# A ConvFFN's up projections by a seven-product scheme over token halves and gate/up columns, in a two-layer float32 decoder

## The chip, the cores and the metric

One core of one Trainium2 chip. The metric is the device time of one execution in microseconds. Before the change it is 1314.91 us, the median of 3 runs (1314.73 to 1315.43).

## What is computed

Two layers on 512 tokens of 1024 features, all float32. Layer 0 mixes by a Mamba-2 scan, layer 1 by differential attention, and behind each mixer stands the same kind of feed-forward block. The change lies in these two blocks alone:

```python
def conv_ffn(x, ln_g, up_w, conv_w, conv_b, down_w):
    u = causal_dwconv(rms_norm(x, ln_g) @ up_w, conv_w, conv_b)
    gate, up = u[..., :FFN_DIM], u[..., FFN_DIM:]
    return (jax.nn.silu(gate) * up) @ down_w
```

`FFN_DIM` is 2816, so `up_w` is 1024 x 5632 and `down_w` is 2816 x 1024 in each layer. `causal_dwconv` is three taps along the tokens and a bias.

## The kernel before

**Features on partitions.** In the feed-forward block every tensor lies with 128 features on the partitions and the 512 tokens along the row. The 2816 gate columns are 22 blocks of 128, and so are the up columns; block p of both makes "pair" p.

**Float32 by three products.** TensorE works on fp32r. Each operand is split into a high piece (ACT copies it to fp32r) and a low piece (DVE subtracts the high piece from the value). One product of values is three matmuls: high by high, high by low, low by high (`mm3`, lines 207 to 210). A weight chunk is 128 x 1024 values: SP loads it into one of three `raw` tiles (line 140), ACT makes `wh` (line 148), DVE makes `wl` (line 159), each from a pool of three buffers. The list `plan` holds all chunks in order of use, and `chunk()` (line 199) splits those up to two ahead of the one in use.

**The up projection** (`products`, line 1002). The chunk `g` or `u` of a pair holds 8 blocks of 128 x 128, one for each 128 input features. They are multiplied with `xgh` and `xgl`, the pieces of the residual stream times its gain; each of the 24 matmuls streams 512 tokens. The RMS factor of each token is not in them: `taps` (line 1013) multiplies the PSUM bank by the row `rr` on DVE while it empties it (line 1021), ACT starts the convolution (line 1022) and DVE does the two other taps (line 1024). The gate goes through Silu on ACT (line 1272), DVE multiplies it with the up half (line 1276).

**The down projection** already runs by a Strassen scheme, over pair parity, token halves and output columns: seven products in place of eight. `operands` (line 1097) makes, for two pairs together, seven 128 x 256 sides in high and low pieces. `down_features` (line 1209, layer 0) streams 256 tokens a matmul and takes the products in the order 5126743; `down_tokens` (line 1129, layer 1) takes 1257634. Sums of weights are made in place: `combine` (line 1065) splits a tile, and then a DMA from POOL adds the next summand to it in DRAM-to-SBUF accumulate mode (`plus`, line 1051). The 22 pairs are done in three parts, `PARTS_D = (0, 6), (6, 14), (14, 22)` (line 32): the up projection of a part, then its share of the down projection (loop at line 1265). In layer 0 the sides for products 5 and 1 need only the even pair of each two; the others also need the odd pair.

**Order.** Within the feed-forward blocks the instruction streams of the engines are put in order at build time by the framework's scheduler, which lets a later instruction go ahead of one whose inputs it does not take to be ready; on the chip each engine then runs its stream in that order. From pair 6 on, layer 0 also stages the scaled key weights for the next mixer (`key_weights_in`, `key_weights_out`, lines 965 and 972): eight loads of 512 KB, and eight stores. Two sets of four PSUM banks, `mm` and `aux`, serve as targets.

Of the kernel before, what the change touches and what calls it, by code (L numbers as in the profile page):

```python
# [18 lines left out]
P = 128  # L19
# [12 lines left out]
PARTS_D = (0, 6), (6, 14), (14, 22)  # L32
# [10 lines left out]
def trunk_kernel(ctx: ExitStack, tc, x, ssm_ln_g, ssm_in_w, ssm_conv_w, ssm_conv_b, ssm_dt_bias,  # L43
# [48 lines left out]
    def ffn_plan(l):  # L92
        for p0, p1 in PARTS_D:
            for p in range(p0, p1):
                plan.append(("g%d_%d" % (l, p), *w_cols(ffn_up_w[l], 0, KB, p * P, P)))
                plan.append(("u%d_%d" % (l, p), *w_cols(ffn_up_w[l], 0, KB, FFN + p * P, P)))
# [28 lines left out]
    state = {"next": 0, "use": 0}  # L125
# [3 lines left out]
    class Weights:  # L129


        def __init__(self, i, behind=None):
# [7 lines left out]
            sync.dma_start(self.cols(self.raw), src)  # L140
# [48 lines left out]
    def emit_chunk():  # L189
        i = state["next"]  # L190
        if i < len(plan):
            state["next"] = i + 1
            if len(plan[i]) == 2:
                state["combine"](plan[i][0], *plan[i][1][1:])
                return
            with tc.issue_after(state["rs"]) if i < 5 else nullcontext():
                Weights(i).split()
# [767 lines left out]
    def key_weights_in(pl, n, behind):  # L965
        t = pl.tile([P, 1024], F32, tag="stage", name="stage%d" % n, bufs=1)
# [31 lines left out]
    def ffn(l, norm, bp, gnext, nnext):  # L998
        with tc.tile_pool(name="ffn_h%d" % l, bufs=1) as hp, tc.tile_pool(name="ffn%d" % l, bufs=1) as fp:
            rr = []  # L1000

            def products(j, p, c=None):
                key = "%s%d_%d" % ("gu"[j], l, p)
                wh, wl = chunk(key)
                ps = mm_bank("ps_" + key)
                for k in range(KB):
                    last = mm3(ps, wh[:, k, :], wl[:, k, :], xgh[k], xgl[k], k == 0, k == KB - 1)
                    if c is not None and k == KB - 2:
                        with tc.issue_after(last):
                            rr.append(norm.row(c))  # L1010
                return ps

            def taps(j, p, ps):
                key = "%s%d_%d" % ("gu"[j], l, p)
                r = rr[0]
                col = lambda t: cf[l][:, 88 * j + 22 * t + p:88 * j + 22 * t + p + 1]
                u = fp.tile([P, T], F32, tag="u", name="u" + key, bufs=3)
                v = fp.tile([P, T], F32, tag="v%d" % j, name="v" + key, bufs=3 if j else 4)
                if nnext is None and key in ("g1_1", "u1_1"):
                    residual(j)  # L1020
                dve.tensor_tensor(out=u, in0=ps, in1=r, op=ALU.mult)  # L1021
                act.activation(v, u, AF.Identity, bias=col(3), scale=col(2))  # L1022
# [713 lines left out]
```

## Time and profile before

| | |
|---|---|
| median of 3 runs | 1314.91 us |
| the profiled execution | 1314.37 us |
| its span, first to last instruction | 1312.7 us |
| layer 0's feed-forward block in it | about 376 to 729 us |
| layer 1's feed-forward block in it | about 959 to 1312 us |
| granted TensorE clock | 1.000 |

The prediction shows the lines on which it rests. The busy time of an engine is the time in which at least one of its instructions was in flight; instructions overlap, so a duration and the distance to the next start differ. A line of a timeline gives the start, the duration, the engine, the line of the kernel, the operation, and output and inputs; in square brackets stands the idle time before it and what ended it.

### The profile page before, as it was taken

The page shows a single profiled execution, that of the slowest core. Times are in us where ns is not written, and L with a number is a line of the kernel's source. Part 1 is how long each engine was busy: PE and PEld are TensorE (multiplying, and loading weights), DVE is VectorE, ACT ScalarE, POOL GpSimd, SP SyncE. Part 2 cuts the span into 40 slices and gives each one's busy share as a digit, 9 for nine tenths or more (in the row PEclk, how much of TensorE's full clock was granted, in tenths as well). Part 3 has the DMA queues.
Part 4 walks back from the last instruction along what each step waited for, and adds up shares of the span by engine and source line. Part 5 has one row for each costly group of instructions (what it writes and reads, how often), then busy time and mean ns, then how long its engine had stood idle before and what let it go on. Part 6 is the DMA issues. An engine that isn't in the chain of part 4 may idle for free.

```text
span 1312.7 us, 18264 instructions
## 1 busy us (share of the span) xinstructions
PE 1307.3 (100%) x6771; PEld 1096.3 (84%) x6771; DVE 1073.9 (82%) x1774; ACT 713.9 (54%) x1156; POOL 177.1 (13%) x244
## 2 busy tenths in 40 slices
PE   9999999999999999999999999999999999999998
PEld 8878888888888998898889887777888888888887
DVE  7889878888888877876888878678778878887886
ACT  6696554743344545543556667777654544544452
POOL 5330200300021401020113210000020100010001
PEclk9999999999999999999999999999999999999999
DMA  7543533432234656774767763222225446453635
GB/s 210 161 152 87 151 99 108 140 96 82 88 91 137 126 144 200 177 163 121 206 174 150 190 131 114 80 65 69 61 81 160 101 116 191 98 96 113 193 64 128
DMA packets 202552, 167.84 MB, mean 128 GB/s; under 512 B 7580, under 2 KB 175904, under 8 KB 202464
## 3 DMA queue, kind: packets, MB, share of 16 engines
q1 hardware_dynamic: 176080, 124.93, 31.9%
q0 software_dynamic: 22928, 36.46, 14.8%
q10 hardware_dynamic: 3456, 5.30, 1.1%
q8 instruction: 53, 0.87, 0.3%
q14 instruction: 35, 0.29, 0.1%
HBM read 160.21 MB, written 6.44 MB: 127 GB/s over the span
## 4 chain that ended last, share of the span: by engine, by line
PE 99%; ACT 1%; DVE 0%; issue 0%; DVEq 0%
PE ps_g L209 6%; PE ps_u L208 6%; PE ps_g L208 6%; PE ps_u L210 6%; PE ps_g L210 6%; PE ps_u L209 6%; PE ps_in L208 5%; PE ps_in L210 5%; PE ps_in L209 5%; PE ps_s L1239 3%; PE ps_s L1244 3%; PE ps_s L1242 3%; PE ps_s L1146 3%; PE ps_s L1141 3%; PE ps_s L1144 3%; PE ps_o L209 2%
## 5 line engine op out<-in xcount | busy, mean ns | idle before, releaser
L208 PE MATMUL ps_u<-xgh,wh_u 128*128 128x512 f32 x352 | 137.4, 390 | 0.0
L209 PE MATMUL ps_g<-xgl,wh_g 128*128 128x512 f32 x352 | 137.2, 390 | 0.0
L208 PE MATMUL ps_g<-xgh,wh_g 128*128 128x512 f32 x352 | 137.0, 389 | 0.0
L210 PE MATMUL ps_u<-xgh,wl_u 128*128 128x512 f32 x352 | 137.0, 389 | 0.0
L210 PE MATMUL ps_g<-xgh,wl_g 128*128 128x512 f32 x352 | 137.0, 389 | 0.0
L209 PE MATMUL ps_u<-xgl,wh_u 128*128 128x512 f32 x352 | 136.9, 389 | 0.0
L208 PE MATMUL ps_in<-xgh,wh_in 128*128 128x512 f32 x304 | 123.0, 404 | 0.0
L210 PE MATMUL ps_in<-xgh,wl_in 128*128 128x512 f32 x304 | 119.7, 394 | 0.0
L209 PE MATMUL ps_in<-xgl,wh_in 128*128 128x512 f32 x304 | 119.2, 392 | 0.0
L209 PEld LDWEIGHTS ps_g<-xgl,wh_g 128*128 128x128 f32 x352 | 66.1, 188 | 14.3 <-DVE xgl L488 0.7
L210 PEld LDWEIGHTS ps_u<-xgh,wl_u 128*128 128x128 f32 x352 | 66.1, 188 | 13.8
L1244 PE MATMUL ps_s<-sl,wh_s 128*128 128x256 f32 x308 | 77.5, 283 | 0.0
L1242 PE MATMUL ps_s<-sh,wh_s 128*128 128x256 f32 x308 | 77.5, 283 | 0.0
L210 PEld LDWEIGHTS ps_g<-xgh,wl_g 128*128 128x128 f32 x352 | 66.1, 188 | 13.7
L208 PEld LDWEIGHTS ps_g<-xgh,wh_g 128*128 128x128 f32 x352 | 66.0, 188 | 13.6
L208 PEld LDWEIGHTS ps_u<-xgh,wh_u 128*128 128x128 f32 x352 | 66.1, 188 | 13.5
L209 PEld LDWEIGHTS ps_u<-xgl,wh_u 128*128 128x128 f32 x352 | 66.1, 188 | 13.5
L1052 POOL DMA_DIRECT2D wz<-in_ffn_down_w_dram x36 | 44.2, 1294 | 235.2 <-DVE wl_s L1080 167.4
L1126 ACT ACTIVATE sh<-vg 128x256 fp32r<-128x256 f32 (+1 forms) x44 | 23.0, 524 | 97.3 <-DVE vg L1276 97.3
L1272 ACT ACTIVATE vg<-vg 128x512 f32<-128x512 f32 x44 | 27.8, 633 | 78.4 <-DVE vg L1024 78.4
L1024 DVE SCALAR_TENSOR_TENSOR vg<-ug,cf,vg 128x511 f32<-128x511 f32 x88 | 65.8, 748 | 5.5 <-ACT vg L1022 4.1
L1021 DVE TENSOR_TENSOR uu<-ps_u,nr_f 128x512 f32<-128x512 f32 x44 | 30.4, 690 | 48.0 <-PE ps_u L210 48.0
(425 smaller groups left out, 3501.2 us busy)
## 6 DMA issues: line engine op xcount, KB each, us to landing
wr_g<-in_ffn_up_w_dram SPq DMA_DIRECT2D x44, 512.0 KB, 3.9
wr_u<-in_ffn_up_w_dram SPq DMA_DIRECT2D x44, 512.0 KB, 3.9
wr_in<-in_ssm_in_w_dram SPq DMA_DIRECT2D x40, 512.0 KB, 3.9
wz<-in_ffn_down_w_dram POOLq DMA_DIRECT2D x27, 512.0 KB, 5.9
m<-cumd POOLq DMA_DIRECT2D x16, 512.0 KB, 4.3
wr_out<-in_ssm_out_w_dram SPq DMA_DIRECT2D x16, 512.0 KB, 3.4
wr_s<-in_ffn_down_w_dram SPq DMA_DIRECT2D x13, 512.0 KB, 3.7
xT<-in_ffn_down_w_dram SPq DMA_DIRECT2D x10, 512.0 KB, 7.0
```

The lines of the kernel that those rows point to most:

```text
L208: pe.matmul(ps, wh, xh, start=start, stop=False)
L209: pe.matmul(ps, wh, xl, start=False, stop=False)
L210: return pe.matmul(ps, wl, xh, start=False, stop=stop).ins
L1021: dve.tensor_tensor(out=u, in0=ps, in1=r, op=ALU.mult)
L1024: dve.scalar_tensor_tensor(out=v[:, s:], in0=u[:, :T - s], scalar=col(2 - s), in1=v[:, s:], op0=ALU.mult, op1=ALU.add)
L1052: pool.dma_start(view(t, nq), source(p0, c, nq, j, i), accum_op=ALU.add)
L1141: pe.matmul(pss[b], h, ws[q][1][:, cols], start=False, stop=end and q == qs[-1], skip_group_check=more)
L1144: pe.matmul(pss[b], h, ws[q][0][:, cols], start=first and q == qs[0], stop=False, skip_group_check=more)
L1146: pe.matmul(pss[b], w, ws[q][0][:, cols], start=False, stop=False, skip_group_check=more)
L1239: pe.matmul(v[:, b], wl[:, q, cols], h, start=False, stop=q == nq - 1, skip_group_check=not opens or b > 0)
L1242: pe.matmul(v[:, b], wh[:, q, cols], h, start=opens and q + b == 0, stop=False, skip_group_check=not opens or b > 0)
L1244: pe.matmul(v[:, b], wh[:, q, cols], w, start=False, stop=False, skip_group_check=not opens or b > 0)
```

## The change

For pairs 6 to 21 two pairs are taken together ("double"). Their four blocks (two of gate, two of up) are computed by seven products over three splits: parity of the 128-feature input blocks, token halves, and gate or up columns. A product is one chunk (4 blocks of input features by 256 columns), multiplied with 256 tokens: 24 matmuls of 256 tokens, times seven. The order is 5126734. Sums and differences of the products are formed in PSUM (products 6, 7 and 4 add to the bank of 1, product 3 to that of 5) and by the instructions that empty the banks.

The inputs of this scheme are linear sums of x, so the token factor has to be in x: during pairs 0 and 1 x is multiplied by gain and `rr` (`normalised`) and split again into the same tiles `xgh` and `xgl` (`split_whole`), and during pairs 2 to 5 the sums of x are formed and split (`x_sums`, `last_sum`). Pairs 2 to 5 still run with 512 tokens a matmul but need no factor any more: their taps read PSUM directly. Pairs 0 to 5 take gate and up interleaved, in chunks of 4 blocks of input features for both (`whole`).

Four of the seven weight sums of a double are made by accumulating DMAs from POOL, as in the down projection: `up_ahead` loads and sums for the next double, `up_combine` splits and then issues the next summand. The parts are now (0, 6), (6, 12), (12, 18), (18, 22), so there is a fourth pass of the down projection. `operands` makes the sums in place in the gate tiles: in a double the even pair contributes its first side, and all sums come with the odd pair; in layer 0 sides 5 and 7 are split together, and 4 and 6 together; in layer 1 sides 6 and 7, and 3 and 5. The staged key weights use a `raw` tile; loads for the down projection hang on given chunks (`hooks`).

```diff
-PARTS_D = (0, 6), (6, 14), (14, 22)
+PARTS_D = (0, 6), (6, 12), (12, 18), (18, 22)
+WHOLE = 6
+STRASSEN_UP = "5126734"
...
+            def normalised(tmp):
+                for j, k, t in tmp:
+                    for i in range(2):
+                        b = 2 * (k + i) + j
+                        g = c2[:, (16 if l == 0 else 24) + b:(16 if l == 0 else 24) + b + 1]
+                        dve.scalar_tensor_tensor(out=t[:, i], in0=xT[b], scalar=g, in1=rr[0],
+                                                 op0=ALU.mult, op1=ALU.mult)
+            def split_whole(j, k, t):
+                pieces(*(x_[:, j, k:k + 2, :] for x_ in xside), t)
+            def x_sums(k, e, o):
+                e0, e1, o0, o1 = (t[:, :, h * 256:(h + 1) * 256] for t in (e, o) for h in range(2))
+                dve.tensor_tensor(out=e0, in0=e0, in1=e1, op=sub)
+                dve.tensor_tensor(out=e1, in0=o1, in1=e1, op=sub)
+                dve.scalar_tensor_tensor(out=o1, in0=o1, scalar=-1.0, in1=e0, op0=ALU.mult, op1=sub)
+                dve.scalar_tensor_tensor(out=o0, in0=o1, scalar=-1.0, in1=o0, op0=ALU.mult, op1=sub)
+                pieces(*(t[:, k:k + 2] for t in sE), e)
+                pieces(*(t[:, k:k + 2] for t in s1), o1)
...
+            def up_combine(key, m, p):
+                if m in "24":
+                    t = wrp.tile([P, 1024], F32, tag="raw", name="wr_" + key)
+                    sync.dma_start(up_view(t), up_source(p, 1, 0 if m == "2" else 1))
+                else:
+                    t = ups[p][m in "17"]
+                wh = wp.tile([P, 1024], F32R, tag="wh", name="wh_" + key)
+                wl = wp.tile([P, 1024], F32R, tag="wl", name="wl_" + key)
+                act.activation(wh, t, AF.Copy)
+                dve.tensor_tensor(out=wl, in0=t, in1=wh.bitcast(F32), op=sub)
+                ready.append((key, up_view(wh), up_view(wl)))
+                more = {"1": (0, 1), "5": (0, 0), "6": (1, 0)}.get(m)
+                if more:
+                    up_plus(t, p, *more)
...
+            def double(p, sides, meanwhile):
...
+                for m in STRASSEN_UP:
+                    wh, wl = chunk("U%d%s_%d" % (l, m, p))
...
+                    for b in range(2):
...
+                        for k in range(4):
+                            pe.matmul(ps[b], wh[:, k, cols], hs[:, k, :], start=not skip and k == 0, stop=False,
+                                      skip_group_check=skip)
+                            pe.matmul(ps[b], wh[:, k, cols], ls[:, k, :], start=False, stop=False,
+                                      skip_group_check=skip)
+                        for k in range(4):
+                            pe.matmul(ps[b], wl[:, k, cols], hs[:, k, :], start=False, stop=k == 3,
+                                      skip_group_check=skip)
+                        if m == "1":
+                            act.activation(ug[:, b, :256], ps[b], AF.Copy)
+                        elif m == "6":
+                            act.activation(ug[:, b, 256:], ps[b], AF.Copy)
+                        elif m == "7":
+                            dve.tensor_tensor(out=uu[:, b, 256:], in0=uu[:, b, 256:], in1=ps[b], op=sub)
+                        elif m == "4":
+                            act.activation(uu[:, b, :256], ps[b], AF.Copy, scale=-1.0)
+                    if m == "5":
+                        act.activation(uu[:, :, 256:], banks["yt"], AF.Copy, scale=-1.0)
+                    elif m == "2":
+                        dve.tensor_tensor(out=ug[:, :, :256], in0=banks["zt"], in1=ug[:, :, :256], op=ALU.add)
+                        meanwhile(ug)
+                    elif m == "3":
+                        dve.tensor_tensor(out=ug[:, :, 256:], in0=banks["yt"], in1=ug[:, :, 256:], op=ALU.add)
+                        ga = [taps(0, p + b, ug[:, b]) for b in range(2)]
+                        for b in range(2):
+                            act.activation(ga[b], ga[b], AF.Silu)
+                for b in range(2):
+                    gated(p + b, ga[b], taps(1, p + b, uu[:, b]), sides)
...
             def operands(p, ga, sides):
...
+                    pieces(sh[:, 0], sl[:, 0], h[:, 0])
+                    return
+                sh, sl, e = sides[-1]
+                pieces(sh[:, 1:3], sl[:, 1:3], h)
...
+                pieces(sh[:, 3:5], sl[:, 3:5], e)
+                pieces(sh[:, 5:7], sl[:, 5:7], h)
...
-                side = {"1": 0, "2": 1, "4": 2, "5": 3, "6": 4, "7": 5, "3": 6}
+                side = {"1": 0, "2": 1, "4": 2, "6": 3, "7": 4, "3": 5, "5": 6}
...
-                side = {"1": 0, "2": 1, "3": 2, "5": 3, "6": 4, "7": 5, "4": 6}
+                side = {"1": 0, "2": 1, "3": 2, "5": 3, "7": 4, "4": 5, "6": 6}
...
+            ps0 = whole(0)
+            ps1 = whole(1)
+            u0 = evac(0, ps0)
...
+            normalised(quarters)
+            for q in quarters[:2]:
+                split_whole(*q)
+            finish(0, (u0[:, 0], u0[:, 1]), sides)
+            for q in quarters[2:]:
+                split_whole(*q)
...
+            pss = whole(3)
+            x_sums(0, tmp[0], tmp[2])
+            ga = finish(3, pss, sides)
...
+            x_sums(2, tmp[1], tmp[3])
+            down_ahead(*parts[0], "z")
+            finish(4, whole(4), sides)
+            pss = whole(5)
+            for k in range(2):
+                last_sum(2 * k, tmp[2 + k])
+            down_ahead(*parts[0], "xy" if l else "x")
+            finish(5, pss, sides)
```

More of the change, by code (lines that the diff above doesn't have):

```diff
@@ L124, in trunk_kernel @@
     ready = []
-    state = {"next": 0, "use": 0}
+    state = {"next": 0, "use": 0, "hooks": {}}
     pin = tc.keep_in_program_order
@@ L1000, in ffn @@
             rr = []
-            def products(j, p, c=None):
-                key = "%s%d_%d" % ("gu"[j], l, p)
[L1004 to L1022, printed above, removed]
+            def whole(p):
+                pss = [(aux_bank if j else mm_bank)("ps_%s%d_%d" % ("gu"[j], l, p)) for j in range(2)]
+                for c in range(2):
+                    wh, wl = (t.rearrange("p (k j) c -> p k j c", j=2) for t in chunk("h%d_%d_%d" % (l, p, c)))
+                    for k in range(4):
+                        for j in range(2):
+                            n = 4 * c + k
+                            last = mm3(pss[j], wh[:, k, j, :], wl[:, k, j, :], xgh[n], xgl[n], n == 0, n == KB - 1)
+                    if p == 0 and c == 0:
+                        col = norm.col()
+                if p == 0:
+                    with tc.issue_after(last):
+                        rr.append(norm.row(col))
+                return pss
```

245 lines of the change are left out of this document (181 added, 64 removed).

## The prediction

> **What bounds the kernel now.** I read the page first, its busy shares and the chain that ended last.
>
> ```profile
> span 1312.7 us, 18264 instructions
> PE 1307.3 (100%) x6771; PEld 1096.3 (84%) x6771; DVE 1073.9 (82%) x1774; ACT 713.9 (54%) x1156; POOL 177.1 (13%) x244
> PE 99%; ACT 1%; DVE 0%; issue 0%; DVEq 0%
> ```
>
> TensorE is never without a matmul, and the chain is 99% its own. Whatever takes matmul time away is worth its full size, as long as nothing else comes late. DVE, at 82%, is the engine nearest behind it. So there are two prices to find: what a matmul takes from start to start, and what the change asks of DVE. Durations of matmuls overlap, so the first price is read from starts in the timeline of PE, at the end of layer 0's first part, where 512-token matmuls give way to 256-token ones.
>
> ```profile
> 439.78 0.39 PE L208 MATMUL ps_u<-xgh,wh_u 128*128 128x512 f32 x1
> ...
> 442.50 0.39 PE L208 MATMUL ps_u<-xgh,wh_u 128*128 128x512 f32 x1
> ...
> 443.18 0.28 PE L1242 MATMUL ps_s<-sh,wh_s 128*128 128x256 f32 x1
> ...
> 448.57 0.28 PE L1242 MATMUL ps_s<-sh,wh_s 128*128 128x256 f32 x1
> ```
>
> Between the first two rows lie 12 steps: 2.72 / 12 = 0.2267 us for 512 tokens. Between the last two lie 45: 5.39 / 45 = 0.1198 us for 256 tokens, 5.7% more than half. DVE next: its groups, then its timeline, where the distances of back-to-back operations can be read, then stretches of layer 0.
>
> ```profile
> L159 DVE TENSOR_TENSOR wl_u<-wr_u,wh_u 128x1024 fp32r<-128x1024 f32 x44 | 54.3, 1235 | 2.6 <-ACT wh_u L148 1.7
> L1024 DVE SCALAR_TENSOR_TENSOR vg<-ug,cf,vg 128x511 f32<-128x511 f32 x44 | 32.8, 746 | 4.1 <-ACT vg L1022 4.1
> L1021 DVE TENSOR_TENSOR uu<-ps_u,nr_f 128x512 f32<-128x512 f32 x44 | 30.4, 690 | 48.0 <-PE ps_u L210 48.0
> ```
>
> ```profile
> 521.46 0.42 DVE L1122 SCALAR_TENSOR_TENSOR sums<-vg,sums 128x256 f32<-128x256 f32 x1
> 521.80 0.42 DVE L1124 TENSOR_TENSOR sums<-vg,vg 128x256 f32<-128x256 f32 x1
> ...
> 522.48 0.68 DVE L1127 TENSOR_TENSOR sl<-vg,sh 128x512 fp32r<-128x512 f32 x1
> 523.08 0.68 DVE L1021 TENSOR_TENSOR ug<-ps_g,nr_f 128x512 f32<-128x512 f32 x1
> ...
> 527.81 1.22 DVE L159 TENSOR_TENSOR wl_u<-wr_u,wh_u 128x1024 fp32r<-128x1024 f32 x1
> 528.95 0.68 DVE L1021 TENSOR_TENSOR uu<-ps_u,nr_f 128x512 f32<-128x512 f32 x1
> ```
>
> ```profile
> 376.00:442.00 66.00, 66.00 (x295) 54.17 (x294) 55.07 (x88) 31.83 (x44) 15.85 (x33) 1.00 0.45 120
> 442.00:474.00 32.00, 32.00 (x261) 31.68 (x261) 26.86 (x37) 15.20 (x18) 5.08 (x4) 1.00 0.73 146
> 474.00:560.00 86.00, 86.00 (x381) 71.21 (x380) 68.57 (x96) 43.38 (x59) 9.58 (x18) 1.00 0.64 179
> ```
>
> The columns are the stretch, its length, and the busy time of PE, PEld, DVE, ACT and POOL with counts, then clock, DMA share and GB/s. Start to start, a DVE operation costs 0.34 us over 256 elements, 0.60 over 512, 1.14 over 1024. DVE is busy 80% of an up stretch (68.57 of 86) and 84% of a down stretch (26.86 of 32).
>
> **Term 1, TensorE in the doubles.** Two pairs took 96 matmuls of 512 tokens, 96 x 0.2267 = 21.76 us. Now they take 7 x 24 = 168 of 256 tokens, 168 x 0.1198 = 20.13. That is 1.63 us less, and in 8 doubles of 2 layers 26.1 us: the most that the change can bring. [...]
>
> **Term 2, DVE in the doubles.** Before, two pairs cost DVE 68.57 / 86.00 x 21.76 = 17.35 us. Added: seven weight splits for four, 3 x 1.14 = 3.42. Emptying the banks: four operations of 512 go (2.40), two of 512 and two of 256 come (1.88), the rest moves to ACT. Taps, product and `operands` keep their element counts. Sum: 17.35 + 3.42 - 0.52 = 20.25 us, against 20.13 of TensorE. In a double DVE becomes the bound, level with the new PE time, and it must feed PE: product 2 can't start before DVE has split it. I take 97% of use, 20.9 us a double, so 0.87 saved and 13.9 in all. Bounds: 20.25 (24.2 saved), and 24 us (36 lost, second rival).
>
> **Term 3, pairs 0 to 5.** Preparing x adds on DVE: 8 multiplications and 4 splits of 1024 (8 x 0.66, by 0.746 less the 0.08 overlap, + 4 x 1.14 = 9.8), the sums (2 x (4 x 0.6 + 1.14 + 0.60) = 8.3) and two splits of 512 (1.2): 19.3. Eight emptyings go (4.8). So 14.5 us more. It can only start with the token factor, whose arrival the DVE timeline shows; ahead of it three stretches show what DVE had left.
>
> ```profile
> 388.90 0.69 DVE L1021 TENSOR_TENSOR ug<-ps_g,nr_f 128x512 f32<-128x512 f32 x1 [1.77 <-ACT nr_f L589]
> ```
>
> ```profile
> 376.00:380.00 4.00, 4.00 (x20) 3.30 (x19) 3.09 (x5) 2.80 (x5) 1.31 (x2) 1.00 0.44 130
> 380.00:384.00 4.00, 4.00 (x20) 2.82 (x19) 3.19 (x5) 1.66 (x3) 0.00 (x0) 1.00 0.43 122
> 384.00:388.00 4.00, 4.00 (x22) 3.31 (x20) 2.75 (x13) 0.00 (x0) 0.00 (x0) 1.00 0.47 139
> ```
>
> Of the 66 us DVE was idle 10.9; 3.0 in these three and 0.9 up to 388.9, so 7.0 are left for 14.5. DVE ends about 7.5 us behind, and the down products wait for its last sides: 8 us a layer, 16 in all. Bounds 3 (half of it slips into the 5.1 idle us of the down stretch) to 13 a layer (pair 2 also waits for the new `xgh`, which can't be written before pair 1 has read the old).
>
> **Term 4, the ends of the parts.** Before, layer 0's first product of the down projection, 5, read sides of even pairs, long finished; the odd pair had 2 products' time. Now 5's side comes from the in-place sums of the odd pair, behind product 4 of the last double, when two pairs have taps, product and sides to do. One such tail of a single `u` stands in layer 1:
>
> ```profile
> 1029.94 0.69 DVE L1021 TENSOR_TENSOR uu<-ps_u,nr_f 128x512 f32<-128x512 f32 x1 [1.79 <-PE ps_u L210]
> ...
> 1039.84 1.23 DVE L1127 TENSOR_TENSOR sl<-sums,sh 128x1024 fp32r<-128x1024 f32 x1
> ```
>
> From 1029.94 to 1041.07 it took 11.1 us, weight splits and adds of the next products in between. The new tail is four taps (3.0), two products (1.3) and some 3 us of sides: 7.3 without anything between. If product 1, which needs the even pair alone (two taps, product, a split, some 3.5 us), goes ahead, 3.5 us are lost; if nothing does, 11. I take 6, nearer to the row without cover, at three ends in layer 0: 18. Layer 1 begins with product 1 and two of three pairs whose sides are old, 12 x 0.2267 = 2.7 us, then 2 and only then 5: I take 1.5 (0 to 3) at three ends, 4.5.
>
> **Term 5, the fourth pass** adds no matmul, but 14 adds of 512 on DVE in layer 0 and 18 in layer 1 (8.4 and 10.8 us). The down stretches have idle time for most of it; the last part is small, and I take 1 us a layer (0 to 2.5): 2.
>
> ACT gains three copies of 1024 and the emptyings, and is far from full at 43.38 of 86; the moved emptyings hide behind other products, unless a copy that waits for a DMA stands before them (second rival). The staging in layer 0 shares three `raw` tiles with two products of seven, which had to serve all before.
>
> **Sum.** -13.9 + 16 + 18 + 4.5 + 2 = +26.6. The profiled execution took 1314.37 us (1312.7 span, 1.7 around it), so 1341.0; the median of the runs lies 0.54 above that execution: **1341.5 us**. With all terms at their low ends the sum is -7.7, with all but the second at their high ends +59; half way to each, that case itself runs from 1324 to 1358.
>
> **Rival one: faster.** DVE's work interleaves so well that doubles run at 20.25 us, the first part loses 3 a layer, and the scheduler sends product 1 ahead so that the ends cost about 1 each: -24.2 + 6 + 3 = -15, 1300 us. For it: the rows at 1029 to 1041 show tail and other work mixed, without a PE stall. Against it: DVE would be over 95% busy through both blocks, which no stretch of 86 us shows.
>
> **Rival two: much slower, by the chain of accumulating loads.** Sum 6 becomes sum 3 in place: the split of 6 must end, POOL issues the DMA, it lands, then 3 is split. ACT's copy, then the issues of DMAs, over the span and in 474 to 560 us:
>
> ```profile
> L148 ACT ACTIVATE wh_u<-wr_u 128x1024 fp32r<-128x1024 f32 x44 | 46.5, 1058 | 37.2 <-PE ps_g L209 31.9 <-PE ps_s L1244 2.9 <-PE ps_s L1146 2.1
> ```
>
> ```profile
> wr_g<-in_ffn_up_w_dram SPq DMA_DIRECT2D x44, 512.0 KB, 3.9
> wz<-in_ffn_down_w_dram POOLq DMA_DIRECT2D x27, 512.0 KB, 5.9
> ```
>
> ```profile
> wz<-in_ffn_down_w_dram POOLq DMA_DIRECT2D x4, 512.0 KB, 6.9
> ```
>
> With three weight buffers 6 can be split once product 5 has ended: ACT 1.06 and DVE 1.14, landing 6.9, ACT and DVE again 2.2: 11.3 us. Product 3 starts four products after 5's end, 4 x 2.88 = 11.5. There is 0.2 us of slack, and in DVE's queue stand up to 7.3 us of the previous double. Each microsecond of lag is one of stall, and ACT, in order, would hold the emptying of 6 behind the waiting copy for 3. It decides from a lag of about 1 us. At 3 us more a double, 24 instead of 20.9, 16 doubles lose 50 us more: 1391. [...]
>
> ```profile
> 446.00:450.00 4.00, 4.00 (x35) 4.00 (x35) 4.00 (x9) 1.95 (x4) 1.83 (x2) 1.00 0.69 100
> 450.00:454.00 4.00, 4.00 (x36) 4.00 (x35) 4.00 (x7) 2.11 (x4) 0.00 (x0) 1.00 0.95 178
> ```
>
> ```profile
> wx<-in_ffn_down_w_dram POOLq DMA_DIRECT2D x2, 384.0 KB, 5.7
> ```
>
> The two accumulating loads issued in 442 to 474 us on `wx`, one of them in these 8 us, landed in 5.7, as elsewhere.
>
> **Rival three: no change.** Terms 3 and 4 come out at their low ends with term 2 as forecast, -13.9 + 6 + 10.5 = +2.6 or less: about 1316.
>
> **Chances.** A measurement tells 0.2%, 2.6 us, from no change. The forecast has 0.47: its DVE sum rests on counted operations and measured distances. Rival two has 0.20, rival one 0.26, rival three 0.07. So faster 0.26, same 0.07, slower 0.67. The range, 1295 to 1388, takes in the forecast's case, rival three, most of rival one and the near half of rival two, so that about 0.15 is left out.
>
> **What would show it.** Right: DVE busy near 1170 us (1074 + 16 x 2.9 + 2 x 14.5 + 8.4 + 10.8), a PE share well under 100%, a chain that holds DVE in the doubles, and PE waiting for `sl` at the ends of layer 0's parts and behind pair 5. Term 1 is wrong if the new matmuls don't start 0.12 us apart. Rival two would show as ACT `wh_U` waiting for the accumulating DMA. The prediction falls if PE stays above 98% busy.

## The result and the profile after

The changed kernel takes 1505.9 us (median of 4 runs, 1505.4 to 1511.3) against 1314.8 before (4 runs, 1314.5 to 1315.4). The ratio is 1.146, with a 95% interval of 1.1435 to 1.1488. So it is slower, as forecast, but by 191 us and not by 27: far above the range. First the page's span and busy shares, and the first line of its chain.

```profile
span 1504.2 us, 21277 instructions
PE 1354.1 (90%) x7923; PEld 1175.5 (78%) x7923; DVE 1151.3 (77%) x1923; ACT 812.8 (54%) x1368; POOL 263.9 (18%) x289
DMA 3%; DVE 3%; issue 2%; PE 1%; ACT 1%; POOL 0%; DVEq 0%; POOLq 0%; ACTq 0%; SPq 0%
```

TensorE was at 100% and is at 90%; DVE has 77 us more work and a lower share. The chain's shares add up to some 10% only, because it can be followed back no further than 1347 us; what can be read in it is that a DMA now stands first. The span's 191.5 us more can be taken apart with the two PE numbers: PE was idle for 5.4 us and is idle for 150.1, which is 144.7. Its busy time went from 1307.3 to 1354.1, though the doubles should have taken 26.1 off it, so 72.9 are left over, by which its matmuls were slowed. So 144.7 + 72.9 - 26.1 = 191.5. What PE and ACT waited for, in sum, times and longest:

```profile
PE ps_U L1146 <- ACT wh_U L1114: 37.0, 13, 6.5
PE ps_s L1289 <- ACT wh_s L1232: 27.9, 11, 7.6
PE ps_U L1146 <- ACT ug L1156: 20.2, 9, 4.6
PE ps_s L1390 <- ACT wh_s L1232: 19.6, 9, 6.3
PE ps_U L1146 <- ACT ug L1154: 14.3, 8, 5.2
```

```profile
ACT wh_U L1114 <- DMA wx<-in_ffn_up_w_dram: 64.7, 17, 7.5
ACT wh_s L1232 <- DMA wz<-in_ffn_down_w_dram: 47.3, 11, 12.2
...
ACT wh_U L1114 <- DMA xT<-in_ffn_up_w_dram: 44.4, 18, 4.6
```

PE waits for ACT, for weight splits (`wh`, in the up and in the down projection) and for emptied banks (`ug`), and hardly for DVE. ACT in turn waits for loads: up weights in `wx` and `xT`, down weights in `wz`, which are the tiles with accumulating loads. How one such wait runs is seen in a double of layer 0, the first behind a down stretch, on POOL (issues at line 1095) and on ACT:

```profile
626.80 1.29 POOL L1095 DMA_DIRECT2D wx<-in_ffn_up_w_dram  x1 [0.22 <-issue]
628.71 1.28 POOL L1095 DMA_DIRECT2D wx<-in_ffn_up_w_dram  x1 [0.61 <-DVE wl_U L1115]
636.64 1.28 POOL L1095 DMA_DIRECT2D wx<-in_ffn_up_w_dram  x1 [6.65 <-DVE wl_U L1115]
```

```profile
634.02 1.06 ACT L1114 ACTIVATE wh_U<-wx 128x1024 fp32r<-128x1024 f32 x1 [6.88 <-PE ps_U L1148]
634.99 0.58 ACT L1162 ACTIVATE uu<-ps_U 128x512 f32<-128x512 f32 x1
635.47 0.38 ACT L1154 ACTIVATE ug<-ps_U 128x256 f32<-128x256 f32 x1
...
642.61 1.06 ACT L1114 ACTIVATE wh_U<-wx 128x1024 fp32r<-128x1024 f32 x1 [3.43 <-DMA wx<-in_ffn_up_w_dram]
```

Sum 6 is issued at 626.80 and split at 634.02, 7.2 us later. The releaser in brackets is PE, but the product whose buffer was needed had ended at 628.2; what came last was the load. Behind the waiting copy, in ACT's order, stand the emptyings of products 5 and 1. Product 6 starts at 635.89. Only its split lets POOL issue sum 3, at 636.64, and product 7 waits for ACT as well: the emptying of product 6 stands behind the copy for 3. Of the 72 us that PE stands still inside the doubles, 34 fall to product 7, in 12 doubles of 16. Then PE itself, at the start of product 7, and two stretches, before and from that start on (columns as in the prediction; the clock is third from the end):

```profile
645.21 0.58 PE L1146 MATMUL ps_U<-sEh,wh_U 128*128 128x256 f32 x1 [4.28 <-ACT ug L1156]
645.59 0.41 PE L1148 MATMUL ps_U<-sEl,wh_U 128*128 128x256 f32 x1
645.80 0.41 PE L1146 MATMUL ps_U<-sEh,wh_U 128*128 128x256 f32 x1
```

```profile
638.00:642.00 4.00, 1.70 (x12) 1.50 (x12) 1.83 (x2) 1.18 (x2) 0.47 (x3) 1.00 0.90 142
642.00:645.20 3.20, 0.00 (x0) 0.00 (x0) 1.23 (x1) 2.55 (x4) 0.45 (x1) 0.98 1.05 358
645.20:648.60 3.40, 3.39 (x16) 3.39 (x17) 0.42 (x2) 1.44 (x2) 0.83 (x1) 0.52 0.86 305
648.60:652.00 3.40, 3.40 (x30) 3.40 (x30) 2.78 (x3) 1.06 (x1) 0.00 (x0) 1.00 1.11 231
```

After 4.28 us of idling the granted clock falls to 0.52 for 3.4 us, and 256-token matmuls start 0.21 us apart where they took 0.12. So this stall cost more than its length, and such stretches are where the 72.9 us come from: the mean granted clock of the execution is 0.954 where it was 1.000, and 0.046 x 1504.2 is some 69 us. Elsewhere it came behind a shorter idle time: behind 1.73 us, from 765.3, the clock was 0.51 from 767.9 to 771.3.

Where the time went by stages, from the first matmul of each stage to that of the next, in us ("ups": the up projection of pairs 6 to 21; "downs": the down stretches behind it; the last stage ends with its last matmul; the remaining 3.7 us lie before and behind; rounding can make a stage 0.1 off):

| stage | before | after | no sums | no sums, no staging | the same, bare ends | plain loads |
|---|---|---|---|---|---|---|
| layer 0, pairs 0 to 5 | 66.6 | 78.2 | 78.3 | 77.5 | 78.1 | 78.3 |
| layer 0, first down | 30.2 | 39.0 | 39.0 | 39.1 | 39.3 | 38.8 |
| layer 0, ups | 174.2 | 237.9 | 185.2 | 161.3 | 161.3 | 198.6 |
| layer 0, downs | 80.6 | 108.9 | 110.3 | 103.2 | 99.4 | 109.1 |
| attention | 231.5 | 241.3 | 241.2 | 241.0 | 240.3 | 239.8 |
| layer 1, pairs 0 to 5 | 70.1 | 70.7 | 70.7 | 70.6 | 70.6 | 70.6 |
| layer 1, first down | 28.8 | 39.0 | 29.7 | 30.1 | 30.0 | 37.5 |
| layer 1, ups | 174.0 | 192.3 | 161.3 | 161.3 | 161.3 | 166.0 |
| layer 1, downs | 76.1 | 112.6 | 102.5 | 102.2 | 87.3 | 108.0 |

The last four columns are experiments, told below. Against before, the ups cost 82.0 us more, the downs 64.8, the first parts with their downs 31.2, and the attention, which nothing of the change touches, 9.8. Of these some 9 can be seen: PE stands still for 2.4 us at 842, waiting for a split on DVE (`wl_q`), and for 3.5 us at 878, ahead of the transposes into `ktq`, and from 880.6 the clock is 0.50 for 6.8 us, which costs up to half of that.

### The profile page after: what moved, and what is told of

Same layout as the page of the kernel before. It is cut to its first block, busy times and chain, and to the rows that moved or that the text cites. A ratio compares the mean times of both kernels' runs of the same rounds, so it can differ in the third digit from the quotient of the medians.

```text
span 1504.2 us, 21277 instructions
## 1 busy us (share of the span) xinstructions
PE 1354.1 (90%) x7923; PEld 1175.5 (78%) x7923; DVE 1151.3 (77%) x1923; ACT 812.8 (54%) x1368; POOL 263.9 (18%) x289
## 5 line engine op out<-in xcount | busy, mean ns | idle before, releaser
L1146 PE MATMUL ps_U<-xgh,wh_U 128*128 128x256 f32 x512 | 135.5, 295 | 37.0 <-ACT wh_U L1114 37.0
L1148 PE MATMUL ps_U<-xgl,wh_U 128*128 128x256 f32 x512 | 133.9, 292 | 0.0
L1146 PEld LDWEIGHTS ps_U<-xgh,wh_U 128*128 128x128 f32 x512 | 102.9, 201 | 39.6 <-ACT wh_U L1114 39.6
L1148 PEld LDWEIGHTS ps_U<-xgl,wh_U 128*128 128x128 f32 x512 | 103.0, 201 | 0.0
L1289 PE MATMUL ps_s<-wh_s,sh 128*128 128x512 f32 x153 | 63.8, 430 | 30.2 <-ACT wh_s L1232 27.9
L1146 PE MATMUL ps_U<-sEh,wh_U 128*128 128x256 f32 x256 | 71.7, 308 | 20.2 <-ACT ug L1156 20.2
L1390 PEld LDWEIGHTS ps_s<-sh,wh_s 128*128 128x128 f32 x308 | 62.7, 206 | 33.8 <-ACT wh_s L1232 22.2
L1151 PE MATMUL ps_U<-xgh,wl_U 128*128 128x256 f32 x512 | 86.1, 293 | 0.8 <-DVE wl_U L1115 0.7
L1114 ACT ACTIVATE wh_U<-xT 128x1024 fp32r<-128x1024 f32 x40 | 42.3, 1059 | 66.6 <-DMA xT<-in_ffn_up_w_dram 44.4
L1151 PEld LDWEIGHTS ps_U<-xgh,wl_U 128*128 128x128 f32 x512 | 74.1, 201 | 2.0 <-DVE wl_U L1115 2.0
L1233 DVE TENSOR_TENSOR wl_s<-wz,wh_s 128x768 fp32r<-128x768 f32 (+2 forms) x50 | 48.0, 965 | 34.9 <-ACT wh_s L1232 34.7
L1146 PEld LDWEIGHTS ps_U<-sEh,wh_U 128*128 128x128 f32 x256 | 53.7, 210 | 22.8 <-ACT ug L1156 22.4
```

The lines of the kernel that those rows point to most:

```text
L1146: pe.matmul(ps[b], wh[:, k, cols], hs[:, k, :], start=not skip and k == 0, stop=False, skip_group_check=skip)
L1148: pe.matmul(ps[b], wh[:, k, cols], ls[:, k, :], start=False, stop=False, skip_group_check=skip)
L1151: pe.matmul(ps[b], wl[:, k, cols], hs[:, k, :], start=False, stop=k == 3, skip_group_check=skip)
L1233: state["low"] = dve.tensor_tensor(out=wl[:, :n], in0=t[:, :n], in1=wh[:, :n].bitcast(F32), op=ALU.subtract).ins
L1289: pe.matmul(pss[b], h, ws[q][0][:, cols], start=first and q == qs[0], stop=False, skip_group_check=more)
L1390: pe.matmul(v[:, b], wh[:, q, cols], h, start=opens and q + b == 0, stop=False, skip_group_check=not opens or b > 0)
```

## The experiments

Theory A: the doubles wait for accumulating loads that land too late. Theory B, the forecast's: DVE is their bound. A time without an interval is one execution; before took 1314.5 to 1315.1 (medians) beside it. The executions of one such kernel lie up to 8 us apart (1468.4 to 1476.7 in the last but one run here), so a few us of a total say nothing, and the stages are read.

**No sums.** In `up_plus` the four accumulating loads of each double are left out.

```diff
             def up_plus(t, p, j, i):
-                pool.dma_start(up_view(t), up_source(p, j, i), accum_op=ALU.add)
+                return
```

> Leaves out the four accumulating loads of every double (the weight sums of five products are then incomplete); all else as changed. Theory A (accumulating loads land late, and ACT, in order, holds PSUM emptyings behind copies that wait for them): the doubles fall from 30.6 us in layer 0 and 24.0 in layer 1 to 20 to 21.5, the half-clock stretches in them go, and the time falls by about 108 us to 1400. Theory B (DVE bounds the doubles): they stay at 24 and more, the time stays above 1450.

Measured: 1403.7. The four loads of each double thus cost 102 us in all. Layer 1's doubles, three at a time:

```profile
1131.30:1191.80 60.50, 60.50 (x505) 60.46 (x505) 54.06 (x75) 40.52 (x63) 1.41 (x2) 1.00 0.34 99
```

Three doubles take 60.5 us, 20.17 each, PE never pauses, and DVE (the third busy time) has 6.4 us to spare in this stretch, with all its work still in the kernel; the last double's tail, some 7 us, falls behind its end. Theory B falls for the doubles.

**Thin sums.** The same loads bring 64 of 256 columns each.

```diff
-                pool.dma_start(up_view(t), up_source(p, j, i), accum_op=ALU.add)
+                pool.dma_start(up_view(t)[:, :, :64], up_source(p, j, i)[:, :, :64], accum_op=ALU.add)
```

> The accumulating loads of the doubles add only 64 of 256 columns: as many DMAs, the same chain and order, a quarter of their bytes (the weight sums are incomplete). If the bytes make them late, the time comes close to that without them, about 1400. If it is the fixed time from issue to landing and the chain, it stays within 40 us of 1506. Theory B: no change.

Measured: 1431.1. With a quarter of the bytes, landing in 3.8 to 4.3 us, 75 of the 102 us are gone, though every wait of the chain is still there.

**ACT's order.** The next splits are emitted behind the emptying of the product at hand, so that no emptying stands behind a copy that waits.

```diff
-                    wh, wl = chunk("U%d%s_%d" % (l, m, p))
+                    wh, wl = taken("U%d%s_%d" % (l, m, p))
+                    done = None
...
+                    refill(done)
```

> Nothing left out: in the doubles a chunk is split only behind the emptying of the bank of the product before it on ACT, so that no emptying stands behind a copy that waits for a DMA. Theory A with the order as its larger half: the 34.5 us that PE waits for the emptyings of products 1 and 6 go, with their half-clock time about 50 us, to 1455. If the lateness of the data alone counts: 1490 to 1510. Theory B: no change.

Measured: 1513.2, nothing gained. The copies then come later themselves, and PE waits for them instead, now ahead of product 3 in 15 doubles of 16. My belief that 50 us would go with ACT's order was wrong. As the new order makes the splits later, and with them the sums, the run doesn't tell how much of the loss is the order's and how much the data's.

**No doubles.** All 22 pairs run as pairs 0 to 5 do.

```diff
-WHOLE = 6
+WHOLE = 22
...
-                        ga = double(p, sides, lambda u, p=p: stage(p, u))
...
+                        ga = finish(p, whole(p), sides)
...
+                        if p == p0 + 2:
+                            down_ahead(p0, n, "zxy" if l else "xz")
```

> All 22 pairs in whole matmuls of 512 tokens as pairs 2 to 5 now, on the normalised x; four parts, the new sides and x sums stay, no seven-product scheme in the up projection. Theory C (x preparation, new sides and the fourth part cost by themselves, as stages 2 to 9 of the changed trace lose 85 us in down projections and 15 in pairs 0 to 5): about 1415. If the down projections lose because the doubles and their loads run into them: about 1335, where the terms 3 to 5 of the forecast put it at 1314.8 + 16 + 22.5 + 2 = 1355 at most.

Measured: 1378.6, between the two values that had been expected. The rest of the change, without the doubles, costs 64 us by itself: layer 0's pairs 0 to 5 and first down take 77.6 and 38.7, its other downs 93.4, layer 1's 82.9, and pairs 6 to 21 take 184.7 and 175.7.

**Plain loads.** The loads of the doubles keep queue, bytes, tiles and order, but overwrite in place of adding.

```diff
-                pool.dma_start(up_view(t), up_source(p, j, i), accum_op=ALU.add)
+                pool.dma_start(up_view(t), up_source(p, j, i))
```

> The changed kernel with the loads of the doubles that add in place turned into plain loads of the same bytes, from the same queue, into the same tiles, in the same order of waits: weights are overwritten in place of summed, so gate and up columns from the seventh pair on are wrong. Theory A1 (it is the adding that makes them land late, 6.3 to 8.5 us against 3.9 to 4.9 of plain ones): they land in 4 to 5 us and most of the 102 us goes, 1420 to 1440. Theory A2 (it is the chain itself, split, issue from POOL, landing, split again, whatever the transfer does): above 1470.

Measured: 1431.7, as theory A1 said. The issues of these loads with count, size and median us to landing, first of the changed kernel, then of this run:

```profile
xT<-in_ffn_up_w_dram POOLq DMA_DIRECT2D x32, 512.0 KB, 6.3
...
wx<-in_ffn_up_w_dram POOLq DMA_DIRECT2D x20, 512.0 KB, 8.5
...
wz<-in_ffn_up_w_dram POOLq DMA_DIRECT2D x12, 512.0 KB, 6.0
```

```profile
xT<-in_ffn_up_w_dram POOLq DMA_DIRECT2D x32, 512.0 KB, 4.2
...
wx<-in_ffn_up_w_dram POOLq DMA_DIRECT2D x20, 512.0 KB, 5.0
...
wz<-in_ffn_up_w_dram POOLq DMA_DIRECT2D x12, 512.0 KB, 4.8
```

With the adding a load lands 1.2 to 3.5 us later, and that alone is 74 of the 102 us. The chain is the same in both; it nearly fits at 4 to 5 us, and doesn't at 6 to 8.5. What goes with the adding is seen in POOL's DMA queue (packets, MB, share of 16 engines), in the changed kernel, with plain loads and with thin sums:

```profile
q0 software_dynamic: 56896, 70.02, 27.8%
q0 software_dynamic: 32320, 70.02, 21.0%
q0 software_dynamic: 56896, 44.85, 20.4%
```

The same bytes take 24576 packets more, 384 for each of the 64 loads: an adding load of 512 KB went as 512 packets of 1 KB, a plain one as 128 of 4 KB, each with 16 below 512 B beside them (the counts by size, less those of the run without these loads). The number of packets alone didn't make these loads late, for the thin ones have as many and landed in 3.8 to 4.3 us. Whether the rest is the adding itself or the smaller packets isn't shown.

**No sums, no staging.** As the first run, and the key weights are not staged beside the doubles; four DMAs behind the last one copy them without their gain, so the keys are others.

```diff
...
             def stage(p, u):
-                if l:
-                    return
+                return
...
+                    for k in range(4):
+                        pool.dma_start(ks[k * 256:(k + 1) * 256, :], kv_w[k * 256:(k + 1) * 256, :D])
```

> The kernel without the accumulating loads of the doubles (1403.7 us), and without the staging of the key weights beside them: the key weights are copied unscaled by four DMAs behind the last double, so keys are computed from weights without their gain. Without sums, layer 0's doubles still took 67.3, 71.3 and 46.6 us, against 60.5, 60.5 and 40.3 in layer 1. Theory A (the staging borrows the three raw tiles, so the plain loads of products 2 and 4 come late): layer 0's doubles fall to 61, 61 and 41, some 22 us, about 1382. Rival (the loads of the next double's first columns come late, whatever is staged): layer 0's doubles stay at 67 or more, 1400 or above. The attention's first loads may move by a few us either way.

Measured: 1379.75. Layer 0's ups fall from 185.2 to 161.3, PE's own time to the decimal, as theory A said (a stall ahead of the block, which this run and two others have, adds 8 us to their totals). Term 1's price of a matmul is exact: 161.3 / 8 = 20.16 us a double, against 20.13.

**Sums, but no staging.** The changed kernel with that edit of the staging alone.

> The changed kernel with all its accumulating loads, but without the staging of the key weights (keys from weights without their gain). In layer 0 the doubles took 91.9, 91.9 and 54.1 us, in layer 1 73.5, 70.9 and 47.9. Theory A (staging and accumulating loads make each other late: the staging explains what layer 0's doubles have above layer 1's): 40 to 50 us less, 1456 to 1466. Rival (the staging adds no more than it did without sums, 24 us): 1480 or above.

Measured: 1489.45 (with the 8 us of that stall in it), and the ups of layer 0 go from 237.9 to 212.6. The staging costs 25 us with the sums and 24 without. Theory A was wrong in that the two don't make each other worse, and layer 0's ups stay 20 us above layer 1's for a reason that I haven't found. The sums of layer 0 in `wx` landed in 8.6 us here and those of layer 1 (`xT`) in 6.1; why isn't known.

**Bare doubles.** The changed kernel without the two shifted taps on DVE in any double.

```diff
-                for s in range(1, 3):
+                for s in range(1, 1 if bare else 3):
...
+                        bare = True
```

> The changed kernel with all its accumulating loads, and without the two shifted taps of the convolution in any double: eight DVE operations of 0.67 us less in each of 16 doubles, 5.4 us of the 20.25 that DVE had to do in one, 86 in all; everything else stays, the chain of the sums too. Theory A (the doubles wait for loads that add in place and land late, and DVE's share in that is the tail at six ends, 19 us by the run with bare ends): 15 to 45 us less, 1460 to 1490. Rival (my second term: DVE is the bound in the doubles, or its queue makes the splits late that the loads wait for): 80 us or more less, below 1425.

Measured: 1475.6. With 80 us of DVE work gone (1151.3 to 1070.9 busy) the time falls by 30, within theory A and far from theory B. Some 22 of the 30 are in the downs behind the doubles; the ups fall by 16.5 in layer 0 and rise by 7.5 in layer 1.

**Bare ends.** On the kernel without sums and staging, the same taps left out in the last double of each part alone.

> The kernel without sums and without staging (1379.75 us), and in the last double of each part without the two shifted taps of the convolution on DVE: eight operations of 0.67 us, 5.4 us less on DVE at each of six ends. Its down stretches behind doubles took 37.0, 37.6, 28.6 us in layer 0 and 37.1, 36.0, 29.1 in layer 1, 4.5 to 8 above PE's own time. Theory T (my fourth term by another path: the tail on DVE holds up the splits, and with them the accumulating loads of the down weights): 3 to 5 us less at each end, 18 to 30 in all, 1350 to 1362. Rival (the down weights' first loads are hooked to a late product and come late whatever DVE does): less than 6 us in all, above 1374.

Measured: 1360.9, 18.9 less. Most of it is in layer 1's downs, 102.2 to 87.3. That the tail on DVE delays the splits there, and these the accumulating loads of the down weights, fits PE's waits for `wh_s`, which fall from 12.2 to 5.5 us in layer 1, but wasn't tested by itself. Layer 0's downs fall by 3.8 only: its waits for the sides (`sh`), 12.9 us, go, and those for `wh_s` grow from 11.8 to 18.8.

**The last two products exchanged**, so that sum 3 has one product more to land. In layer 0 the last double of each part then has a down load written over the tile of sum 3 too early, so that product 3 there takes other weights.

```diff
-STRASSEN_UP = "5126734"
+STRASSEN_UP = "5126743"
```

> The changed kernel with the last two products of a double exchanged, 5126743: nothing is left out, and sum 3 has one product more (2.9 us) to be accumulated and split. Theory A (products wait for accumulating loads that are late by a few us): up to 2.9 us less in each double that waits for product 3, so 20 to 45 us off 1505.9: 1460 to 1485. Rival (sum 6 and the first sum of the next double are as late as sum 3, and the lag only moves there): less than 10 us either way.

Measured: 1479.8, 26 less, most of it in layer 1 (ups 192.3 to 179.8, downs 112.6 to 103.4). Theory A holds at the low end.

**Bias ranges behind the down loads.** `bias_ranges` is emitted behind `down_ahead`.

> The changed kernel with the bias ranges' work on POOL emitted behind the accumulating loads of layer 0's first down projection, in place of ahead of them. Theory A (those loads waited for POOL, and product 5 of the down projection for them): the first down stretch falls from 39.0 to about 31 us, 1498. Rival (it waits for the sides that DVE makes late, my term 3): the stretch stays within 2 us of 39.0, and the time at 1505.

Measured: 1508.3, no change. But the run didn't test the theory: POOL still did two of its three accumulating loads of that stage behind the bias work, since the order is made by the scheduler and not by the text.

**Order and bias mended.** The product order with the down loads hooked to product 3, and `bias_ranges` behind pair 0, where POOL is idle.

```diff
-STRASSEN_UP = "5126734"
+STRASSEN_UP = "5126743"
...
-            finish(0, (u0[:, 0], u0[:, 1]), sides)
+            ga = finish(0, (u0[:, 0], u0[:, 1]), sides)
+            if not l:
+                bias_ranges(fp, ga)
...
-                hooks["U04_%d" % last] = second
+                hooks["U03_%d" % last] = second
```

> The changed kernel, complete, with products 4 and 3 of a double exchanged (the last down loads of layer 0 hooked to product 3 then), and the bias ranges' work on POOL behind pair 0 in place of pair 3, where POOL has nothing else to do. In the run that only emitted it behind the down loads, POOL still did it ahead of two of the three accumulating loads it issued there, so that run didn't test it. Theory A: the doubles as with the order alone (87, 90, 54; 65, 68, 46) and the first down stretch 31 to 33 in place of 39 to 40.5: about 1470. Rival (my third term alone: DVE ends late and the down projection waits for it and for loads that wait for its splits): the first down stretch stays at 38 or more, about 1480.

Measured: 1465.7. Layer 0's pairs 0 to 5 go from 78.2 to 73.3 and its first down from 39.0 to 36.1, so the bias work on POOL cost some 8 us. The total is as theory A said, though the down stretch stayed above its 31 to 33. In the changed kernel one sees the bias work in POOL's last count, then in PE's first:

```profile
444.00:448.00 4.00, 4.00 (x19) 3.30 (x18) 0.69 (x1) 1.16 (x2) 3.89 (x20) 1.00 0.00 0
448.00:452.00 4.00, 3.22 (x15) 2.33 (x13) 0.00 (x0) 0.00 (x0) 3.37 (x4) 1.00 0.37 43
452.00:456.00 4.00, 0.37 (x1) 0.37 (x2) 0.39 (x1) 1.26 (x3) 0.00 (x0) 0.74 0.94 149
```

POOL works through the bias copies up to 448, DVE and ACT have little to do, two accumulating loads are issued only then, and PE stands still nearly all the time from 452 to 456.

**Down weights first, by a later hook.** In layer 1 the next double's loads are hooked to product 3 of the down projection, not 6.

> The changed kernel, complete, with the loads for the next part's first double hooked one product later in layer 1, to product 3 of the down projection in place of 6, so that in POOL's queue the last accumulating load of the down weights stands ahead of the double's. Theory Q (that load waited behind the double's: POOL issued it at 1173.96 us and ACT had its data only at 1184.6): layer 1's first down stretch 39.0 goes to 31, the two others lose up to 8 each, and the first double behind each part starts up to 3 us later: 10 to 22 us less in all, 1484 to 1496. Rival (contention for bytes, whatever the order, or DVE's tail): the three stretches stay within 2 us, 1500 to 1510.

Measured: 1508.4. Again the edit didn't bring the order about: POOL still issued the double's load first, at 1173.05 us. It tests nothing.

**All mended**, with that hook.

> The complete kernel with the order 5126743, the bias ranges behind pair 0, and the down weights' loads ahead of the next double's in layer 1: the run with order and bias took 1465.7. Theory Q: 10 to 22 less, 1444 to 1456. Rival: within 5 of 1465.7. On no theory does it come near the kernel before: without sums, without staging and with bare ends it was 1360.9.

Measured: 1473.0, median of 4 runs; ratio to before 1.121, interval 1.1185 to 1.1235. As the hook does nothing, it is the run with order and bias again, and the best complete kernel that I found.

**Down weights first, made certain.** With the same hook, the double's loads are issued behind the last accumulating load of the down weights.

```diff
...
-                        up_ahead(p1)
+                        with tc.issue_after(state["plus"]) if l else nullcontext():
+                            up_ahead(p1)
```

> The changed kernel, complete, with the loads for the next part's first double issued only behind the last accumulating load of the down weights in layer 1, so that this one now does stand ahead in POOL's queue, which the run with the later hook did not bring about. Theory Q (the down weights' load waits behind the double's in one queue): the first down stretch of layer 1 falls from 39.0 to 31, the next two from 42.4 and 42.5 to 35 to 38, less up to 3 us a part by which the double starts later: 10 to 22 us less in all, 1484 to 1496. Rival (bytes or DVE's tail): within 5 of 1505.9.

Measured: 1493.5. Layer 1's downs fall from 39.0, 42.4 and 42.5 to 32.1, 34.5 and 34.9, 22.4 together, as theory Q said; the doubles behind them give 11 back (192.3 to 203.4). In the changed kernel (POOL, then ACT):

```profile
1173.21 1.30 POOL L1095 DMA_DIRECT2D xT<-in_ffn_up_w_dram  x1 [7.86 <-DVE xr L1295]
1173.96 2.69 POOL L1199 DMA_DIRECT2D wz<-in_ffn_down_w_dram  x2
```

```profile
1184.59 1.06 ACT L1232 ACTIVATE wh_s<-wz 128x1024 fp32r<-128x1024 f32 x1 [11.00 <-DMA wz<-in_ffn_down_w_dram]
```

The down weights' load, issued 0.75 us behind the double's, has its data split 10.6 us later. In this run it goes first, and is split within 6 us:

```profile
1170.69 2.13 POOL L1199 DMA_DIRECT2D wz<-in_ffn_down_w_dram  x2 [6.66 <-DVE wl_s L1233]
1172.10 2.05 POOL L1095 DMA_DIRECT2D xT<-in_ffn_up_w_dram  x1
```

```profile
1176.63 1.06 ACT L1232 ACTIVATE wh_s<-wz 128x1024 fp32r<-128x1024 f32 x1 [4.39 <-PE ps_s L1286]
```

Now it is the double's load, issued second at 1172.10, that is late: ACT waits for a DMA into `xT` and splits at 1183.14, 11.0 us after that issue.

## Why the prediction was wrong

That the kernel got slower had been forecast, but the cause was another one, so the right direction was in part luck. Against the forecast's terms: the doubles -13.9, measured 82.0 more (in the ups); pairs 0 to 5 with their down 16, measured 31.2; the ends and the fourth pass 24.5, measured 64.8; the attention nothing, measured 9.8.

**Term 1** was right to 2%: where nothing is late, 25.6 us are saved of 26.1. But in the changed kernel nowhere is nothing late.

**Term 2 is the step that failed.** "In a double DVE becomes the bound", with 20.9 us a double. DVE's sum was right: 3 x 20.25 = 60.75, and the row of the run without sums shows 54.06 with the tail of the last double, some 7 us, beyond its end. The conclusion was wrong, because DVE may carry that tail into the down stretch: over the doubles of a part it is no bound, though the tail costs time behind them (terms 4 and 5). A double without late loads takes 20.17 us and not 20.9. What bound the doubles in its place was the chain of accumulating loads, 83.7 us in the ups of both layers, and the staging with 23.9: 83.7 + 23.9 - 25.6 = 82.0. The chain I had put into rival two, with 0.20.

**Rival two** had the mechanism, step for step: the split of 6, POOL's issue, the landing, the split of 3, the emptyings held behind a waiting copy. It had computed a slack of 0.2 us with a landing of 6.9. In layer 0 the new loads on `wx` took 8.5. In layer 1 they landed in 6.3, less than reckoned, and PE still stood still in every double. A double that starts at 1192.47, on POOL, ACT and PE:

```profile
1198.95 1.28 POOL L1095 DMA_DIRECT2D xT<-in_ffn_up_w_dram  x1 [4.86 <-DVE wl_U L1115]
```

```profile
1205.06 1.06 ACT L1114 ACTIVATE wh_U<-xT 128x1024 fp32r<-128x1024 f32 x1 [4.62 <-DMA xT<-in_ffn_up_w_dram]
1206.03 0.37 ACT L1156 ACTIVATE ug<-ps_U 128x256 f32<-128x256 f32 x1
```

```profile
1206.44 0.39 PE L1146 MATMUL ps_U<-sEh,wh_U 128*128 128x256 f32 x1 [2.30 <-ACT ug L1156]
```

Sum 3 is issued at 1198.95 and split from 1205.06 on; the emptying of product 6 comes behind that copy, and product 7 starts 2.3 us late. Rival two's price, 3 us a double, was too small: the sums cost 52.7 us in layer 0's ups and 31.0 in layer 1's, 83.7 / 16 = 5.2 a double, plus 18 net in the downs. Missing were the half clock behind many of the stalls, and that the doubles' loads and the down weights' share POOL's one queue. Which of the two parts of its reasoning, the late data or ACT's order, is the larger isn't shown. Nor is it shown that a busy DVE makes such loads late: plain loads from the same queue beside the same DVE landed in 4.2 to 5.0 us, and in the run with bare doubles, with 80 us less work on DVE, the adding loads landed in 6.6 to 7.6, on `wx` 0.9 us sooner and on the two other tiles 0.6 later.

**Term 3** (16 us, bounds 6 to 26) was 31.2, and without what it hadn't priced it came near only in sum, by luck. In layer 0 pairs 0 to 5 with their down cost 20.4 us more, some 8 of them by the bias work, which I hadn't counted, as I had not read on POOL what the moved down loads were now behind; so some 12 where 8 were forecast. In layer 1 they cost 10.8, of which 9.3 go without the sums, so 1.5 where 8 were forecast. Nor was the wait the one forecast: in layer 0 PE waited not for the sides but for splits of down weights (`wh_s`), 4.4 us up to 455.6 behind the bias work and 6.3 up to 463.1. That second one waited for a load into `wx`, the tile from which DVE still split x at 457.76.

**Terms 4 and 5** (24.5 us) were 64.8. For layer 0 the order of magnitude was right, 28.3 where 19 were forecast. The "0 to 3" at an end of layer 1 was not: 36.5 where 5.5 were forecast. I had covered the sides with product 1, and forgotten that the same tail can hold up the weights' splits, and with them the loads that add in place. Bare ends give 14.9 back there, the queue's order some 15.5 in the first two of the three stretches. They were measured in different kernels and may overlap, so they can't be added.

**Not forecast:** the staging, 24 to 25 us, which I had named ("shares three `raw` tiles with two products of seven, which had to serve all before") and costed at nothing. Its loads, stores and 16 copies on ACT were there before, with a tile of their own; new is that it takes a `raw` tile from products 2 and 4. That this is what costs is likely, but the runs leave out the staging as a whole. And the attention, 8 to 10 us in the variants of the table.

Rivals one and three fell with PE at 90%. Of what I had named as signs, DVE's 1151 (near 1170), the distance of 0.12 us, and ACT `wh_U` waiting for the accumulating DMA came. PE waiting for the sides at the ends of layer 0's parts hardly did: three waits for their high piece `sh`, 6.7 us in all; mostly it waits for `wh_s`.

What stays open: why the two stalls in the attention come, why layer 0's ups are slower than layer 1's even without the staging, and what makes the weight splits late in layer 0's later downs (99.4 with bare ends, where before took 80.6).

## What to carry to other kernels

A chain of dependent transfers has to be priced end to end with the landing time that it will have under its own load (8.5 us on `wx`, where 6.9 was reckoned), and a computed slack near zero is no fit: with 0.2 us of it, PE stood still in every double of layer 1. Whether an engine is the bound is asked over the stretch across which its backlog may be carried, not over one step. And a price for a stall of TensorE has to hold the half clock that may follow it: here it added 73 us to 145 us of idle time.

## What the runs showed of the hardware

The doubles' accumulating loads of 512 KB from POOL landed in 6.0 to 8.5 us (medians by tile), as 512 packets of 1 KB, plain ones in their place from the same queue in 4.2 to 5.0, as 128 packets of 4 KB. Of two accumulating loads issued 0.75 us apart in that queue the second had its data split 10.6 us after its issue, against 5.9 when it went first. And the clock: idling of 4.28 us was followed by 3.4 us at 0.52 of full speed; the rows from 638 to 642 us, after idling of 1.4 and 1.6 us, still show 1.00, while 1.73 us from 765.3 on were followed by 3.4 us at 0.51. In the changed kernel's trace PE stood still for 4 us and more ten times (4.28 to 7.64 us), and each time the clock in the 2 us behind it was 0.50.
